# A hybrid encoder layer: scan factors on GpSimd, turns and casts at later places, final sums in two banks

## The chip, the cores and the metric

The kernel runs on one core of a Trainium2 chip. The metric is the device time of one execution in microseconds (us); three executions were timed and the median counts. A further execution was recorded by the hardware profiler, and all durations below come from that one.

The engines of the core are named as in the profile: PE is TensorE (matrix products; PEld is its loading of weights, which overlaps), DVE is VectorE, ACT is ScalarE, POOL is GpSimd, SP is the engine whose queue issues most transfers. Each engine works through its own list of instructions strictly in order, and an instruction that waits holds back everything behind it in its list.

## The reference, cut to what matters

One layer over a prompt of 512 tokens and a sample group of 64 tokens, 1024 wide, in float32:

```python
h = x + W_out [ GDN(n) ; DiffAttn(n) ],  n = rmsnorm(x)      # gated-delta scan, 4 heads of 128
h = h + MemCrossAttn(rmsnorm(h), mk, mv)                     # mk = m @ wk, mv = m @ wv, m = rmsnorm(mem), 256 tokens
h = h + W2 relu(W1 rmsnorm(h))^2                             # 1024 -> 4096 -> 1024
y = rmsnorm_final(h)

# one chunk of the scan, S is the recurrent state of a head
vn = u_c - w_c @ S
o  = qg_c @ S + qk_c @ vn
S  = S * gl_c + kd_c.T @ vn
oa = rmsnorm(o, gdn_norm) * silu(z)                          # a row norm of every head's output, then the gate
```

The queries and keys of the scan are l2-normed rows; the outputs include the memory keys and values, the state and the two rows of caches.

## The kernel before, in words

Everything is held transposed, with features on the 128 partitions and the 576 tokens in the free dimension, and every large product is made of three: weights and inputs are split into a high part in a rounded format (`wh`, `u`) and a low part that holds the rest (`wl`). ACT casts the high part, DVE subtracts to get the low part. Products accumulate in banks of PSUM: three banks `pr` for the large projections, two `ba` for turns (transposes) and small products, and one each of `gs`, `g0` and `g1`, which the scan and its preparation use.

The stages follow each other in the program: norm and input projection; the gated-delta part (`gdn_prep`, `gdn_scan`, `gdn_scan_sample`, some 130 to 290 us into the execution) with the projections of the difference attention as other work for PE beside it; the difference attention (`diff_head`); memory keys and values; output projection; memory attention; the feed-forward layer (`ff1_pair` for its first product, a Strassen-like scheme with seven products of half size); the final norm.

A tile framework schedules the instructions: from the order in which they are written, priorities (`tc.high_priority`) and estimated costs it lays out one list for each engine, so an instruction written early may stand late in its engine's list. `tc.issue_after(x)` asks for a place behind instruction x; `tc.keep_in_program_order` pins one. Where a tile has one buffer (`on`, `r`, `vn`; `on` and `r` even share it) or one bank (`gs`), its next use waits for the last reader.

What the change touches:

- `gdn_prep` (lines 672 to 716) makes for each of five chunks (0 to 3 of the prompt with four blocks, 4 of the sample with two) the row sums `s8` of squared keys and queries, their power -1/2 on POOL (`rpow`, line 208), and from them `nk`, `rq`, `rq2` on DVE (lines 711 to 713), tiny tiles of 128x4. It also solves a triangular system by levels of products in the banks `g0` and `g1` (lines 749 to 783): each level goes PE, ACT (line 762), DVE (763), PE, DVE (770, 771), ACT (769) and back to PE.
- `gdn_scan` (810 to 843) runs the recurrence of one chunk, then `normed` (797 to 808): ACT squares the output that stands in bank `gs` (801), DVE sums the rows (802), makes the factor (803, 804), POOL takes its power (208), DVE multiplies (806) and scales the output out of the bank into `on` (808). Then PE turns `on` back in bank `gs` (`gs<-ident,on`) and DVE applies the gate (842). All of this is written before the preparation of the chunk after next.
- `diff_head` ends with the factor of its own norm (lines 1103 and 1104) inside `finish`.
- The memory keys: a loop over two weights and two halves f; each half makes eight products of 256 tokens in two `pr` banks. For the keys, each half is then turned back (lines 1158 to 1165) through four fillings of a `ba` bank, `ba<-ident,u`, each split by ACT (1131) and DVE (1132).
- `split` (1422 to 1428) casts and subtracts weights of the second feed-forward product: `w2h` on ACT (1426), `w2l` on DVE (1427). The first of them are cast while `ff1_pair(1)` runs, whose partial products are copied out of their banks by `keep` on ACT (1462).
- `final_roots` (1570 to 1581) sums squares over the features with products against a column of ones, `ba<-ones,accq` and `ba<-ones,tm`, then root and scaling.

## Time and profile before

| | us |
|---|---|
| timed runs, median (lowest to highest) | 979.41 (978.93 to 979.56) |
| the profiled execution | 979.89 |
| its span, first to last instruction | 978.2 |
| PE busy | 960.9 |
| PEld busy | 889.0 |
| DVE busy | 691.4 |
| ACT busy | 537.4 |
| POOL busy | 57.5 |
| moved by DMA | 96.01 MB, mean 98 GB/s |

Read it so: a busy time is the time in which an engine had at least one instruction under way. The profiled execution is 1.7 us longer than its span (start and end lie outside), and 0.48 us longer than the median of the timed runs. Of the span, 17.3 us are without PE, and 7.9 of these fall behind the end of the last product at 970.34 us, when the results are scaled and stored. In a row of the timeline the columns are start, duration, engine, line, operation, output and inputs, shape, and in brackets how long the engine had idled before and what ended that. A row of the waits gives the waiting engine and line, what it waited for, and total us, number and longest wait.

### The profile page before, as it was taken

Reading aid. Unit: us, or ns where it says so; the run is one execution under the profiler, and the core shown is the slowest. Engines: PE = TensorE matmul, PEld = TensorE weight load, DVE = VectorE, ACT = ScalarE, POOL = GpSimd, SP = SyncE. Lnnn points to the kernel's source line nnn. Section 1 sums busy time; section 2 is a strip of 40 time slices with the busy share of each in tenths; the row PEclk is TensorE's granted clock in tenths of the full one; section 3 lists DMA queues with packets and bytes.
Section 4 is the critical chain, followed back from the end, with each engine's and each line's share of the span. In section 5 each row is a group of like instructions: output and inputs, shape, how many; then the busy total and the mean of one; then the engine's idle time right before and its main releaser. Section 6 shows DMA issues by size and latency. Waiting matters only on the chain.

```text
span 978.2 us, 16971 instructions
## 1 busy us (share of the span) xinstructions
PE 960.9 (98%) x6399; PEld 889.0 (91%) x6399; DVE 691.4 (71%) x1540; ACT 537.4 (55%) x1218; POOL 57.5 (6%) x125
## 2 busy tenths in 40 slices
PE   9999999999999999999999999999999999999996
PEld 7999999898888878999999998999999999999996
DVE  6655777867767676666657797567867779978674
ACT  7665785444557675445445567665544445545444
POOL 3441020101000000000000000000000000000000
PEclk9999999999999999999999999999999999999998
DMA  7432432121654656341121423322222223233202
GB/s 216 124 124 76 114 105 66 33 55 40 179 132 132 231 159 197 86 130 44 52 58 44 141 70 93 87 87 86 87 87 86 86 87 87 86 88 86 65 23 97
DMA packets 124915, 96.01 MB, mean 98 GB/s; under 512 B 6204, under 2 KB 112846, under 8 KB 124322
## 3 DMA queue, kind: packets, MB, share of 16 engines
q1 hardware_dynamic: 124466, 94.28, 33.2%
q8 instruction: 50, 0.82, 0.3%
q10 hardware_dynamic: 368, 0.66, 0.2%
q14 instruction: 31, 0.25, 0.1%
HBM read 79.93 MB, written 9.75 MB: 92 GB/s over the span
## 4 chain that ended last, share of the span: by engine, by line
PE 86%; DVE 5%; ACT 3%; issue 2%; DMA 2%; POOL 1%; POOLq 0%; ACTq 0%; DVEq 0%; SPq 0%
PE pr L107 53%; PE g L107 11%; PE ba L107 10%; PE gs L107 6%; PE ba L113 3%; PE g L113 2%; DMA raw<-in_w_ff_dram 1%; DMA r<-in_w_ff_dram 1%; POOL tg L208 1%; DVE wl L162 1%; DMA raw<-in_w_mem_o_dram 1%; ACT wh L161 0%; DVE w L1326 0%; PE gs L113 0%; DVE on L808 0%
## 5 line engine op out<-in xcount | busy, mean ns | idle before, releaser
L107 PE MATMUL pr<-u,wh 128*128 128x320 f32 (+2 forms) x1240 | 326.5, 341 | 1.4 <-DVE zr L195 0.9
L107 PEld LDWEIGHTS pr<-u,wh 128*128 128x128 f32 x1240 | 211.9, 188 | 16.9 <-DVE zr L195 1.1
L107 PE MATMUL pr<-u,wl 128*128 128x256 f32 (+1 forms) x816 | 225.8, 301 | 0.0
L107 PEld LDWEIGHTS pr<-u,wl 128*128 128x128 f32 x816 | 150.0, 189 | 2.2 <-DVE wl L388 0.2
L162 DVE TENSOR_TENSOR wl<-raw,wh 128x1024 fp32r<-128x1024 f32 x65 | 79.5, 1223 | 56.0 <-ACT wh L161 55.8
L161 ACT CAST wh<-raw 128x1024 fp32r<-128x1024 f32 x65 | 68.2, 1050 | 59.9 <-PE pr L107 43.9
L107 PE MATMUL pr<-u,w2h 128*128 128x320 f32 (+1 forms) x384 | 98.5, 340 | 0.0
L1426 ACT CAST w2h<-r 128x512 fp32r<-128x512 f32 x56 | 34.7, 620 | 89.0 <-PE pr L107 85.8
L107 PE MATMUL pr<-f,w2h 128*128 128x320 f32 (+1 forms) x288 | 74.4, 341 | 0.2 <-DVE u L1513 0.2
L107 PEld LDWEIGHTS pr<-u,w2h 128*128 128x128 f32 x384 | 65.0, 188 | 4.5 <-ACT u L1509 0.3
L107 PE MATMUL pr<-u,w2l 128*128 128x256 f32 (+1 forms) x256 | 65.1, 295 | 0.0
L1511 DVE TENSOR_TENSOR u<-u,pr 128x256 f32<-128x256 f32 x96 | 42.4, 450 | 17.0 <-PE pr L107 16.3
L107 PE MATMUL ba<-u,wl 128*128 128x288 f32 x360 | 53.0, 296 | 0.9 <-ACT keep L1462 0.9
L107 PEld LDWEIGHTS pr<-f,w2h 128*128 128x128 f32 x288 | 48.7, 188 | 4.2 <-issue 1.4
L107 PEld LDWEIGHTS ba<-u,wl 128*128 128x128 f32 x360 | 49.2, 188 | 1.7 <-ACT keep L1462 1.6
L107 PE MATMUL pr<-f,w2l 128*128 128x256 f32 (+1 forms) x192 | 48.8, 295 | 0.0
L107 PEld LDWEIGHTS pr<-u,w2l 128*128 128x128 f32 x256 | 46.9, 188 | 1.5
L208 POOL TENSOR_TENSOR tiny<-tiny,nhalf 128x1 f32<-128x1 f32 (+4 forms) x10 | 9.1, 913 | 643.4 <-DVE tiny L1579 531.5
L1427 DVE TENSOR_TENSOR w2l<-r,w2h 128x512 fp32r<-128x512 f32 x56 | 38.5, 688 | 11.2 <-ACT w2h L1426 10.9
L107 PE MATMUL pr<-wh,u 128*128 128x512 f32 x128 | 41.4, 398 | 0.0
L1471 ACT ACTIVATE c<-c 128x288 f32<-128x288 f32 x48 | 20.6, 443 | 29.5 <-DVE c L1470 29.5
L107 PEld LDWEIGHTS pr<-f,w2l 128*128 128x128 f32 x192 | 35.2, 188 | 1.1
(551 smaller groups left out, 2022.2 us busy)
## 6 DMA issues: line engine op xcount, KB each, us to landing
raw<-in_w_ff_dram SPq DMA_DIRECT2D x36, 512.0 KB
raw<-in_w_in_dram SPq DMA_DIRECT2D x28, 512.0 KB
r<-in_w_ff_dram SPq DMA_DIRECT2D x56, 256.0 KB
raw<-in_w_mem_k_dram SPq DMA_DIRECT2D x8, 512.0 KB
raw<-in_w_mem_v_dram SPq DMA_DIRECT2D x8, 512.0 KB
raw<-in_w_out_dram SPq DMA_DIRECT2D x8, 512.0 KB
raw<-in_w_mem_q_dram SPq DMA_DIRECT2D x8, 512.0 KB
raw<-in_w_mem_o_dram SPq DMA_DIRECT2D x8, 512.0 KB
```

The lines of the kernel that those rows point to most:

```text
L107: i = nc.tensor.matmul(out, lhsT, rhs, start=start, stop=stop, skip_group_check=skip_group_check)
L113: i = nc.tensor.transpose(out, in_, ident[:n, :n])
L161: A.copy(wh, raw)
L162: V.tensor_tensor(wl, raw, wh.bitcast(F32), ALU.subtract)
L208: G.tensor_tensor(out, in_, bc(nhalf[: in_.shape[0], 0:1], list(in_.shape)), ALU.pow)
L1426: A.copy(wh, src)
L1427: V.tensor_tensor(wl, src, wh.bitcast(F32), ALU.subtract)
L1471: A.activation(c, c, AF.Relu)
L1511: V.tensor_tensor(am, am, b, ALU.add)
```

## The change

Five edits, none of which changes what is computed:

1. In `gdn_prep` the three tiny operations for `nk`, `rq`, `rq2` go from DVE to POOL, directly behind the power.
2. In `normed` the two operations before the power and the one behind it go from DVE to POOL; `normed` becomes a generator that stops before the scaling. `gdn_scan` returns the rest (scaling, turn, gate) as `finish`, and the caller runs it after the preparation of the next chunk has been written; for chunk 3 at once. The sample's scan stops at the same point.
3. In `diff_head` the factor's first operation goes to POOL, and for the last head both are written before `finish`. That last `finish` moves from behind the memory keys into the first half of the memory values.
4. The turns of the memory keys are written inside the next half's product loop (at kc = 1) instead of behind their own half.
5. The non-urgent `split`s of the second feed-forward weights get `issue_after` the last subtraction of `ff1_pair(1)`; and the last sums with `more` go to a bank of their own, with one more small DVE operation (`scalar_tensor_tensor`) that adds the two.

```diff
--- before.py
+++ after.py
@@ -684,10 +684,15 @@
         if c == 0:
             turned.update(summed=nc.cur_bb.bb.instructions[-1])
         V.tensor_scalar(s8, s8, EPS, None, ALU.add)
-        rpow(r8, s8)
         brk = tiny([P, nb], "tg")
         V.reciprocal(brk, s8[:, :nb])
         V.tensor_tensor(brk, brk, be, ALU.mult)
+        nk, rq2 = tiny([P, nb], "tg"), tiny([P, nb], "tg")
+        rq = r8[:, nb:]
+        rpow(r8, s8)
+        G.tensor_tensor(nk, s8[:, :nb], r8[:, :nb], ALU.mult)
+        G.tensor_scalar(rq, rq, P ** -0.5, None, ALU.mult)
+        G.tensor_tensor(rq2, rq, rq, ALU.mult)
 
         if c in grows:
             bg = v4(grows[c], nb)
@@ -706,11 +711,6 @@
         KQ4, vb4 = sb("KQ"), sb("vb")
         KQ = KQ4[:, :nb]
         V.tensor_tensor(KQ, bkq, gam, ALU.mult)
-        nk, rq2 = tiny([P, nb], "tg"), tiny([P, nb], "tg")
-        rq = r8[:, nb:]
-        V.tensor_tensor(nk, s8[:, :nb], r8[:, :nb], ALU.mult)
-        V.tensor_scalar(rq, rq, P ** -0.5, None, ALU.mult)
-        V.tensor_tensor(rq2, rq, rq, ALU.mult)
         bv = each(tr, vblk)
         vb = vb4[:, :nb]
         V.tensor_tensor(vb, bv, nk.unsqueeze(2).to_broadcast(wide), ALU.mult)
@@ -800,10 +800,11 @@
         for R, src in parts:
             A.activation(out[R], src, AF.Square)
         V.tensor_reduce(so, out, AX.X, ALU.add)
-        V.tensor_tensor(so, so, q["rq2"], ALU.mult)
-        V.tensor_scalar(so, so, 1.0 / P, EPS, ALU.mult, ALU.add)
+        G.tensor_tensor(so, so, q["rq2"], ALU.mult)
+        G.tensor_scalar(so, so, 1.0 / P, EPS, ALU.mult, ALU.add)
         rpow(co, so)
-        V.tensor_tensor(co, co, q["rq"], ALU.mult)
+        G.tensor_tensor(co, co, q["rq"], ALU.mult)
+        yield
         for R, src in parts:
             V.tensor_tensor(out[R], src, co[R].unsqueeze(2).to_broadcast(list(src.shape)), ALU.mult)
 
@@ -837,10 +838,15 @@
         b = each(lambda o, h: mm(o, q["kd"][:, h, :], vn[:, h, :]), "ba")
         S = next_state(c, S, b)
         on = sb("on", 1)
-        normed(q, 4, [(slice(0, P), bo)], on)
-        bt = each(lambda o, h: tr(o, on[:, h, :]))
-        V.scalar_tensor_tensor(cq, bt, gn, zs[:, :, L], ALU.mult, ALU.mult)
-        return S
+        norm = normed(q, 4, [(slice(0, P), bo)], on)
+        next(norm)
+
+        def finish():
+            next(norm, None)
+            bt = each(lambda o, h: tr(o, on[:, h, :]))
+            V.scalar_tensor_tensor(cq, bt, gn, zs[:, :, L], ALU.mult, ALU.mult)
+
+        return S, finish
 
     def gdn_scan_sample(q, S):
 
@@ -882,8 +888,10 @@
         yield
         on4 = sb("on", 1)
         on = on4[:, :nb]
-        normed(q, nb, [(R, bo[R, :, i, :]) for i, R in enumerate(own)], on)
+        norm = normed(q, nb, [(R, bo[R, :, i, :]) for i, R in enumerate(own)], on)
+        next(norm)
         yield
+        next(norm, None)
         bt = each(lambda o, i: tr(o, on[:, i, :]), P)
         out = on4[:, nb:].rearrange("p b n -> p (b n)").rearrange("p (h t) -> p h t", h=H)
         V.scalar_tensor_tensor(out, bt[:, : H * DEC].rearrange("p (h t) -> p h t", h=H), gn, zsample, ALU.mult, ALU.mult)
@@ -899,14 +907,17 @@
                 A.copy(mhi, src)
                 V.tensor_tensor(mlo, src, mhi.bitcast(F32), ALU.subtract)
 
-    S = None
+    S, behind = None, lambda: None
     prepared = [gdn_prep(*chunks[0])]
     for c, _, L in chunks[:4]:
         prepared.append(gdn_prep(*chunks[c + 1]))
         if c == 0:
             turn_memory()
             project_z()
-        S = gdn_scan(c, L, prepared[c], S)
+        behind()
+        S, behind = gdn_scan(c, L, prepared[c], S)
+        if c == 3:
+            behind()
     nc.sync.dma_start(o_gdn_p[0, 0].rearrange("h k v -> k h v"), S)
     oa = pair(2, F32R)
     for h in range(H):
@@ -1099,9 +1110,16 @@
             A.activation(pr[1][:, :P], po, AF.Square, accum_out=so[:, t : t + 1])
             A.copy(on[:, t, :], po)
 
+        def factors():
+            G.tensor_scalar(so, so, 1.0 / P, EPS, ALU.mult, ALU.add)
+            rpow(co, so)
+
+        if h == H - 1:
+            factors()
+
         def finish():
-            V.tensor_scalar(so, so, 1.0 / P, EPS, ALU.mult, ALU.add)
-            rpow(co, so)
+            if h < H - 1:
+                factors()
             V.tensor_tensor(on, on, co.unsqueeze(2).to_broadcast([P, 5, P]), ALU.mult)
             b, b2 = bank(), bank()
             for t in range(4):
@@ -1134,6 +1152,21 @@
     mkv = pair(1, F32R)
     mkT, mv, tokens = view(mkv, 0, KT, NMEM), view(mkv, 1, 2, D), view(e3, 1, 2, D)
     mkl, mvl = lows("At0", "At1", "Dt0", "Dt1"), lows("Y0", "Y1", "B1", "B1")
+    turn_keys = lambda: None
+
+    def key_turns(f, dst):
+        def turn_keys():
+            for i in range(2):
+                b = bank()
+                for j in range(2):
+                    m = 4 * f + 2 * i + j
+                    for t in range(2):
+                        tr(b[:, j * 256 + t * P : j * 256 + (t + 1) * P], dst[:, t, m * P : (m + 1) * P])
+                m = 4 * f + 2 * i
+                split_turned(mkT[:, m : m + 2, :], mkl[m // 2].rearrange("p (j n) -> p j n", j=2), b)
+
+        return turn_keys
+
     for w, out in ((w_mem_k, o_mk), (w_mem_v, o_mv)):
         dst = tokens
         for f in range(2):
@@ -1141,6 +1174,10 @@
             bs = [bank("pr") for _ in range(2)]
             for kc in range(4):
                 wt = split_weights(w[0, 256 * kc : 256 * kc + 256, fs], [P, 2, 512])
+                if kc == 1:
+                    turn_keys()
+                    if out is o_mv and f == 0:
+                        finish()
                 for k in (2 * kc, 2 * kc + 1):
                     for t in range(2):
                         ts_ = slice(t * P, (t + 1) * P)
@@ -1154,18 +1191,8 @@
                 if out is o_mv:
                     A.copy(mv[:, t, fs], dst[:, t, fs])
                     V.tensor_tensor(mvl[2 * t + f], dst[:, t, fs], mv[:, t, fs].bitcast(F32), ALU.subtract)
-            if out is o_mk:
-                for i in range(2):
-                    b = bank()
-                    for j in range(2):
-                        m = 4 * f + 2 * i + j
-                        for t in range(2):
-                            tr(b[:, j * 256 + t * P : j * 256 + (t + 1) * P], dst[:, t, m * P : (m + 1) * P])
-                    m = 4 * f + 2 * i
-                    split_turned(mkT[:, m : m + 2, :], mkl[m // 2].rearrange("p (j n) -> p j n", j=2), b)
             nc.sync.dma_start(out[0, 0].rearrange("(b p) h d -> p b (h d)", p=P)[:, :, fs], dst[:, :, fs])
-            if out is o_mk and f == 1:
-                finish()
+            turn_keys = key_turns(f, dst) if out is o_mk else lambda: None
             if out is o_mv and f == 0:
                 ob = pair(5, F32R)
                 for h in range(H):
@@ -1422,7 +1449,7 @@
     def split(src, tag, bufs, urgent):
         shape = list(src.shape)
         wh, wl = (ft(tag + x, shape, bufs, F32R) for x in "hl")
-        with tc.high_priority() if urgent else ExitStack():
+        with tc.high_priority() if urgent else tc.issue_after(put_last[1]):
             A.copy(wh, src)
             V.tensor_tensor(wl, src, wh.bitcast(F32), ALU.subtract)
         return wh, wl
@@ -1433,6 +1460,7 @@
         return split(raw, "w2", 3, urgent)
 
     NG, SCALED = 8, 5
+    put_last = {}
 
     def ff1_pair(p, sx):
         ws = parts.pop(p)
@@ -1492,6 +1520,7 @@
         put(1, N1, s3, s5)
         product(4, x, False)
         put(1, N0, x[:, :NH], None)
+        put_last[p] = nc.cur_bb.bb.instructions[-1]
         if p + 1 < 2 * NG:
             split_pair(p + 1)
         if p + 2 < 2 * NG:
@@ -1573,10 +1602,14 @@
         r, r2 = tiny([P, 8]), tiny([P, 8])
         for i, t in enumerate(ts):
             q0, n = QT[t]
-            mm(b[:, t : t + 1], accs[0][:, q0 : q0 + n], ones[:, 0:1], stop=more is None, pin=pin and i == 0)
-            if more is not None:
-                mm(b[:, t : t + 1], more[:, q0 - 256 : q0 - 256 + n], ones[:, 0:1], start=False)
+            mm(b[:, t : t + 1], accs[0][:, q0 : q0 + n], ones[:, 0:1], pin=pin and i == 0)
         V.tensor_scalar(r[:, c], b[:, c], 1.0 / D, EPS, ALU.mult, ALU.add)
+        if more is not None:
+            b = bank()
+            for t in ts:
+                q0, n = QT[t]
+                mm(b[:, t : t + 1], more[:, q0 - 256 : q0 - 256 + n], ones[:, 0:1])
+            V.scalar_tensor_tensor(r[:, c], b[:, c], 1.0 / D, r[:, c], ALU.mult, ALU.add)
         rpow(r2[:, c], r[:, c])
         return r2
 
```

How the lists of the engines stand before and after at three places (a row is line, operation, output and inputs, shape; the lines of the changed kernel are some numbers higher).

First, DVE's list at the norm of chunk 0, `tg` being the factor and `on` the output. Before:

```order
L802 TENSOR_REDUCE tg_1892<-on_1891 128x4
L771 TENSOR_TENSOR Dt_214_1517<-Dt_214_1517,g_228_1582 128x16x16
L803 TENSOR_TENSOR tg_1892<-tg_1892,tg_1334 128x4
L676 TENSOR_TENSOR kd_1914<-g_274_1909,kdc 128x512
L804 TENSOR_SCALAR tg_1892<-tg_1892 128x4
L806 TENSOR_TENSOR tg_1893<-tg_1893,tg_1279 128x4
L808 TENSOR_TENSOR on_1891<-gs_1879,tg_1893 128x512
```

Now:

```order
L802 TENSOR_REDUCE tg_1892<-on_1891 128x4
L676 TENSOR_TENSOR kd_1907<-g_273_1902,kdc 128x512
L809 TENSOR_TENSOR on_1891<-gs_1879,tg_1893 128x512
L783 TENSOR_SCALAR X_1515<-g_234_1614 64x4x64
L679 TENSOR_REDUCE tg_1901<-B_275_1909 128x4
```

Three tiny rows left DVE's list, and the scaling (line 809) stands two places behind the row sum instead of six; the tiny rows follow each other in POOL's list, around the power of line 208.

Second, PE's list ahead of the turn of chunk 3, `gs<-ident,on`. Before:

```order
L107 MATMUL pr_3365<-u_94,wl_3362 128x256
L107 MATMUL pr_3365<-u_94,wh_3361 128x512
L107 MATMUL g_410_2450<-Y_395_2397,X_2396 128x128
L107 MATMUL pr_3365<-u_94,wl_3362 128x256
L113 MATMUL gs_2511<-ident,on_2501 128x128 x4
```

Now:

```order
L107 MATMUL ba_2492<-vn_2481,kd_2126 128x128
L113 MATMUL ba_2644<-ident,u_78 128x128 x2
L107 MATMUL g_406_2431<-Y_394_2390,X_2389 128x128
L113 MATMUL ba_2684<-ident,u_78 128x128 x2
...
L113 MATMUL ba_2719<-ident,zr_2716 128x128 x2
L113 MATMUL g_408_2438<-ident,Y_394_2390 128x128
L107 MATMUL g_408_2438<-Dt_395_2391,B_407_2436 128x128
L113 MATMUL ba_2750<-ident,zr_2748 128x128 x2
...
L113 MATMUL gs_2511<-ident,on_2501 128x128 x4
L107 MATMUL pr_3363<-u_93,wh_3359 128x512
```

Before, the turn stood among the products of the next projection, `pr`. Now it stands ahead of the first of them, behind turns, small products and levels of the solve (`...` marks rows left out).

Third, PE's list at the last turns of the memory keys, `ba<-ident,u`, and of the last head, `ba<-ident,an`. Before:

```order
L113 MATMUL ba_4211<-ident,u_76 128x128 x4
L113 MATMUL ba_4295<-ident,u_76 128x128 x4
L107 MATMUL pr_4322<-wh_4326,u_1250 128x512 x2
L107 MATMUL pr_4322<-wl_4327,u_1250 128x512
...
L113 MATMUL ba_4302<-ident,u_76 128x128 x4
L107 MATMUL pr_4323<-wh_4344,u_1250 128x512
L113 MATMUL ba_4313<-ident,an_3948 128x128 x4
```

Now:

```order
L107 MATMUL pr_4299<-wl_4303,u_1250 128x512
L113 MATMUL ba_4324<-ident,u_76 128x128 x4
L113 MATMUL ba_4331<-ident,u_76 128x128 x4
L107 MATMUL pr_4298<-wh_4320,u_1250 128x512 x2
L107 MATMUL pr_4298<-wl_4321,u_1250 128x512
...
L113 MATMUL ba_4339<-ident,an_3948 128x128 x4
```

Before, three fillings of `ba` followed each other closely and a fourth soon after; now they come in pairs, with a projection's products between the pairs, and the head's turn last.

## The prediction

> **What bounds the kernel now.** I read the page first: its line of busy times, then the chain of work that ended last.
>
> ```profile
> PE 960.9 (98%) x6399; PEld 889.0 (91%) x6399; DVE 691.4 (71%) x1540; ACT 537.4 (55%) x1218; POOL 57.5 (6%) x125
> PE 86%; DVE 5%; ACT 3%; issue 2%; DMA 2%; POOL 1%; POOLq 0%; ACTq 0%; DVEq 0%; SPq 0%
> ```
>
> PE is the bound: 960.9 of a span of 978.2 us, and the change leaves PE's number of products as it is. All that can be won are the 17.3 us without PE, and what can be lost is new waiting of PE. So the next view is the table of busy time in windows of 20 us, of which these are the windows that lack PE and that the edits touch (columns: window, length, busy time of PE, PEld, DVE, ACT, POOL with numbers of instructions, granted clock, DMA).
>
> ```profile
> 120.00:140.00 20.00, 19.40 (x137) 18.05 (x136) 13.86 (x38) 18.26 (x32) 3.90 (x3) 1.00 0.43 142
> 160.00:180.00 20.00, 19.07 (x156) 16.85 (x155) 14.11 (x41) 8.63 (x18) 3.25 (x4) 1.00 0.15 40
> 180.00:200.00 20.00, 19.64 (x153) 18.50 (x152) 18.29 (x50) 8.62 (x20) 2.71 (x2) 1.00 0.15 41
> 220.00:240.00 20.00, 19.45 (x151) 17.53 (x149) 13.86 (x44) 6.92 (x20) 2.32 (x3) 1.00 0.10 27
> 240.00:260.00 20.00, 18.91 (x126) 16.69 (x125) 16.50 (x45) 12.47 (x35) 1.27 (x1) 1.00 0.75 199
> 280.00:300.00 20.00, 19.20 (x123) 17.45 (x122) 14.90 (x53) 11.20 (x41) 1.84 (x2) 1.00 0.36 103
> 360.00:380.00 20.00, 18.92 (x88) 15.34 (x88) 14.42 (x18) 11.85 (x16) 0.00 (x0) 1.00 0.54 171
> 580.00:600.00 20.00, 19.11 (x141) 18.55 (x140) 14.52 (x26) 15.34 (x37) 0.00 (x0) 1.00 0.42 119
> 600.00:620.00 20.00, 19.68 (x132) 18.43 (x131) 15.08 (x27) 13.54 (x33) 0.00 (x0) 1.00 0.45 132
> ```
>
> These nine lack 0.60, 0.93, 0.36, 0.55, 1.09, 0.80, 1.08, 0.89 and 0.32 us. That caps the gains: 4.33 us in the gated-delta windows (120 to 300 us), 1.08 us at the memory keys, 1.21 us in the feed-forward layer. The clock is granted in full in all of them. The view of waits says who ends these gaps.
>
> ```profile
> PE gs L113 <- DVE on L808: 1.3, 2, 0.8
> PE gs L107 <- DVE on L808: 0.7, 1, 0.7
> PE ba L113 <- DVE At L1132: 1.1, 1, 1.1
> PE ba L107 <- ACT keep L1462: 1.2, 2, 0.9
> DVE tg L711 <- POOL tg L208: 3.2, 3, 1.5
> DVE tg L806 <- POOL tg L208: 2.8, 3, 1.1
> ```
>
> Three waits of PE are for the scaling of a scan's norm (line 808), one is for the keys' split, two are for `keep`. And DVE itself stood 6.0 us for POOL's powers.
>
> **The scan's factors and last steps.** The timeline of chunk 0's norm, from the squares to the turn:
>
> ```profile
> 168.76 0.60 ACT L801 ACTIVATE on<-gs 128x512 f32<-128x512 f32 x1 [0.15 <-PE gs L107]
> 169.02 0.97 PEld L107 LDWEIGHTS ba<-vn,kd 128*128 128x128 f32 x8
> 169.54 0.68 DVE L802 TENSOR_REDUCE tg<-on 128x4 f32<-128x512 f32 x1
> 170.46 0.16 DVE L803 TENSOR_TENSOR tg<-tg,tg 128x4 f32<-128x4 f32 x1
> 171.14 0.16 DVE L804 TENSOR_SCALAR tg<-tg 128x4 f32<-128x4 f32 x1
> 171.38 1.01 POOL L208 TENSOR_TENSOR tg<-tg,nhalf 128x4 f32<-128x4 f32 x1 [10.12 <-DVE tg L804]
> 172.43 0.16 DVE L806 TENSOR_TENSOR tg<-tg,tg 128x4 f32<-128x4 f32 x1 [1.12 <-POOL tg L208]
> 172.62 0.69 DVE L808 TENSOR_TENSOR on<-gs,tg 128x512 f32<-128x512 f32 x1
> 173.37 0.55 PE L113 MATMUL gs<-ident,on 128*128 128x128 f32 x3 [0.75 <-DVE on L808]
> ```
>
> Between the end of the row sum (170.22) and the scaling (172.62) lie 2.40 us: two tiny operations on DVE that stand behind other work there, the power, a third. DVE loses 34 tiny rows (20 of two inputs, 14 of one) at about 0.16 us, 5.4 us in all, plus the 6.0 us of waiting. DVE is not the bound, so this is worth only what PE waits for it.
>
> The trace has no multiplication of 128x4 on POOL. The nearest rows by lines:
>
> ```profile
> L208 POOL TENSOR_TENSOR tg<-tg,nhalf 128x4 f32<-128x4 f32 x5 | 5.3, 1067 | 52.3 <-DVE tg L804 47.6 <-DVE tg L686 4.7
> L461 POOL COPY cst<-p 128x3 f32<-128x3 f32 x11 | 8.1, 733 | 23.0 <-ACT p L322 23.0
> L462 POOL COPY cst<-p 128x3 f32<-128x3 f32 x11 | 2.0, 183 | 1.0 <-ACT p L323 1.0
> ```
>
> A copy of 128x3 takes 0.73 us after a pause of POOL and 0.18 us right behind another; a power of 128x4 takes 1.07. So one tiny operation lies between 0.18 and 1.07 us. I take 0.6 for the first (a pause precedes it) and 0.25 for each later one, near the copies, since neither has the power's arithmetic: 0.6 + 0.25 + 1.07 + 0.25 = 2.2 us against 2.40 now. The chain from row sum to scaling stays as long as it was; by the bounds it is 1.6 to 4.3 us. GPSIMD Engine Reference of the Trainium skill (section Engine selection) speaks against the move: elementwise work belongs on VectorE, with GpSimd about twice as slow for two inputs. By it each moved operation would take an estimated 0.32 us, the chain 2.0, and the slower rival below would lose its price.
>
> What does change is DVE's list: at chunks 0 to 2 the scaling (809) now stands two or three places behind the row sum, so DVE stands idle for it, 2.2 less 0.7 to 1.1 us of work between, some 1.3 us each. Queued behind are steps of the other chunk's solve and preparation. At chunks 0 to 2 PE has projection products (`pr`) beside these; behind the outputs of chunk 0, PE's list to its turn holds some 5 us of work (ten products of scan and solve at about 0.24 each, by the 0.97 us of the row's eight loads, two to a product; ten turns at half of that; eighteen shorter ones), against 0.15 + 0.60 + 0.18 + 0.68 + 2.2 + 0.7 = 4.5 us of chain. I leave 0.1 of the 0.75 us there and 0.2 of the 0.55 at chunk 2: **-1.0**. The 0.60 and 0.36 us at 120 to 140 and 180 to 200 us lie where DVE waited for the powers of the preparation; I give back 0.4 of the 0.96: **-0.4** (bounds 0 and -0.96). At the sample's norm the wait of 0.69 us for line 808 has as many products ahead as chain: **-0.2**.
>
> Chunk 3 is the bad place, and it speaks against the change. Today's gap near its norm is another one:
>
> ```profile
> 243.63 1.27 POOL L208 TENSOR_TENSOR tg<-tg,nhalf 128x4 f32<-128x4 f32 x1 [13.76 <-DVE tg L804]
> 244.19 0.42 DVE L195 TENSOR_TENSOR zr<-pr,zr 128x256 f32<-128x256 f32 x1
> 244.67 0.50 PE L107 MATMUL pr<-u,wh 128*128 128x512 f32 x1 [0.85 <-DVE zr L195]
> ```
>
> PE waits 0.85 us for a bank that `zr` (195) empties late. Now the scaling of chunk 3 stands directly ahead of `zr` on DVE, and the turn directly ahead of the first `pr` on PE. From the last product of the outputs to the turn the chain is 4.5 us plus the hop to PE, 4.6. PE has behind those outputs four products `ba<-vn,kd` (0.97 us as above), four of the solve (0.24 each) and some thirteen turns (0.12 each), and little more: 3.5 us. PE is short of 1.1 us. Ahead of it, I take 0.4 us as lost at the hops of the solve and the scan, which had projection products between them. The 0.85 goes: **+0.65**. The bounds: -0.85, if other waits of the solve fall into the same time, and +3.6, if the tiny operations cost as much as a power (2.1 us more) and the levels of the solve are bare (0.85 more). That power took 1.27 us here, while DVE worked beside it, and 1.01 at chunk 0, while DVE waited; the same page (section Key points) says that GpSimd shares its SBUF interfaces with VectorE and collides with instructions of two SBUF inputs, and the two rows agree; by it chunk 3's chain would be an estimated 0.25 us longer, and the sum -2.15.
>
> **Memory keys.**
>
> ```profile
> 361.76 0.65 PE L113 MATMUL ba<-ident,u 128*128 128x128 f32 x4 [1.08 <-DVE At L1132]
> ```
>
> The fourth filling waits 1.08 us for one of two `ba` banks. In the new list two fillings, then twenty products `pr`, then two fillings stand: no third one waits. The turns read copies (1153) made well ahead. The last head's turn moves behind its power by more. **-1.0** (bounds -1.08 and +0.5, if the turned half, now written among the next half's products, meets a bank that the difference attention still holds).
>
> **Second feed-forward weights.**
>
> ```profile
> 589.39 0.62 ACT L1426 CAST w2h<-r 128x512 fp32r<-128x512 f32 x1 [2.07 <-DMA r<-in_w_ff_dram]
> 591.25 0.40 ACT L1462 COPY keep<-ba 128x288 f32<-128x288 f32 x1
> 591.70 1.06 PE L107 MATMUL ba<-u,wl 128*128 128x288 f32 x6 [0.89 <-ACT keep L1462]
> 607.37 1.34 PE L107 MATMUL ba<-u,w 128*128 128x288 f32 x8 [0.27 <-ACT keep L1462]
> ```
>
> ACT stands 2.07 us for the weights of a cast (1426), the `keep` comes late, PE waits 0.89. The edit is meant for this, but the lists show that it does not reach ACT: the same cast stands between the same two rows there. The instruction it names is DVE's, and only DVE's subtractions move behind it, by some 10 us, with the buffers `r` they free and three loads that wait for these; the products that need them come 10 us later still. So the 0.89 us stay. ACT's `keep` at 606 us does stand earlier, ahead of two casts of weights: the 0.27 goes, **-0.3** (bounds -0.6 and +0.5, where a copy that now stands behind frees a `pr` bank late at 615 us).
>
> **Final sums.**
>
> ```profile
> 968.67 0.30 PEld L107 LDWEIGHTS ba<-ones,tm 128*128 128x128 f32 x2 [0.16 <-ACT tm L1201]
> 969.59 0.36 PE L107 MATMUL ba<-ones,tm 128*128 128x1 f32 x2
> 969.99 0.16 DVE L1579 TENSOR_SCALAR tiny<-ba 128x3 f32<-128x3 f32 x1 [1.87 <-PE ba L107]
> ```
>
> Six sums before and six now, 0.23 us apart (968.67 to 969.59 in four steps). Two of them now run ahead of the turns, so PE's weight load no longer waits 0.16 us for `tm`; the added DVE row replaces the one on the path, which moves into the 1.87 us of idling. **-0.15** (bounds -0.3 and +0.2).
>
> **The sum.** -1.0 - 0.4 - 0.2 + 0.65 - 1.0 - 0.3 - 0.15 = -2.4 us on the profiled execution (979.89, span 978.2): 977.5. The timed median is 0.48 us lower; from 979.41 the same step gives 977.0.
>
> **The rivals.**
>
> - The waits only change place. For it: chunk 3's list, and that the scan is one chain of hops whatever PE does beside it. Against it: the keys' 1.08 us have nothing to do with the scan. The scan then takes 1.6 us more than in the sum, so that its gains are gone, 978.6, and with the keys' gain at half 979.1.
> - Slower, by one mechanism: a tiny operation on POOL costs as much as the power, 1.0 us. The chain is then 4.2 us instead of 2.2. DVE, standing in order at the scaling, is idle 3.3 us at each chunk; PE's turns of chunks 0, 2, 3 and the sample come 2.0 us later with nothing left to cover it, 8 us, less some 3 us that the projections behind cover when they come in between: +5 against the sum, 982.0. It decides from about 0.6 us for each operation. For it: the power row of 1.07, and 0.73 for a copy. Against it: the copies of 0.18.
> - Everything is covered, because DVE is freer and its later work no longer stands behind powers: the chunk 3 term is -0.85 instead of +0.65 and the 0.96 us go whole: 974.9.
> - The casts go later on ACT after all, and the 0.89 us go too: 976.1.
>
> **How the numbers follow.** Forecast 0.50, own range 975.2 to 978.5; waits moved 0.17; slower 0.16; all covered 0.12; casts 0.05. What a measurement of this kernel can tell from no change is about 0.2%, 2.0 us. Faster by more than that (below 977.45): 0.12 + 0.05, 0.36 of the forecast's 0.50, and 0.02 of the moved waits: 0.55. Slower (above 981.37): 0.16, and 0.02 of the moved waits: 0.18. Between: 0.27. The range takes in the moved waits, part of the slower case and most of the covered one: 974.0 to 981.2.
>
> **What would show it.** Right: no wait of PE for the scaling at chunks 0 and 2 (now 0.75 and 0.55), none for the keys' split at 361 us, DVE's waits for POOL gathered at line 809, an unchanged wait of 0.89 us for `keep` near 590 us, PE short by about 1.5 us ahead of chunk 3's turn. Wrong: tiny POOL rows above 0.6 us; PE idle over 4 us in 160 to 300 us; or a new gap at the memory values. Most in doubt is the stretch of chunk 3.

## The result and the profile after

| | before | changed |
|---|---|---|
| median of 22 runs each, us | 979.69 | 978.34 |
| lowest to highest | 978.48 to 981.85 | 977.08 to 979.61 |
| span of the profiled execution | 978.2 | 976.5 |

The ratio is 0.9986 with a 95% interval of 0.998 to 0.9992: 1.4 us faster, clear of no change, but under the 2.0 us that was named as what can be told. The forecast was 2.4 us faster; the sign and the range held, while three of its larger terms did not. By the span from first to last instruction the gain is larger: the 22 executions have a median span of 976.05 us, and the kernel before had 977.8 to 978.2 in the three series of the experiments below. The time outside the span was 1.7 to 2.0 us in these executions of the kernel before and 1.9 to 3.3 in the changed one; why is not known. The page of the changed kernel begins:

```profile
span 976.5 us, 16991 instructions
PE 961.3 (98%) x6399; PEld 890.0 (91%) x6399; DVE 689.2 (71%) x1507; ACT 537.4 (55%) x1218; POOL 64.9 (7%) x159
```

PE did the same work. So the windows of 20 us tell again where it stood still (third number: PE busy; what is missing to 20 us is idle time).

```profile
120.00:140.00 20.00, 19.71 (x140) 18.54 (x139) 13.90 (x34) 17.64 (x32) 5.90 (x9) 1.00 0.52 159
160.00:180.00 20.00, 19.90 (x163) 17.72 (x162) 12.69 (x31) 9.98 (x20) 2.40 (x7) 1.00 0.11 27
180.00:200.00 20.00, 19.69 (x151) 18.76 (x149) 17.46 (x39) 8.76 (x19) 4.01 (x8) 1.00 0.25 63
220.00:240.00 20.00, 18.06 (x146) 16.34 (x145) 14.79 (x41) 7.44 (x20) 3.56 (x9) 1.00 0.10 27
240.00:260.00 20.00, 19.31 (x134) 16.89 (x133) 14.87 (x43) 12.81 (x40) 1.61 (x4) 1.00 0.62 171
280.00:300.00 20.00, 19.54 (x121) 17.36 (x120) 14.79 (x48) 11.43 (x38) 2.41 (x5) 1.00 0.35 94
340.00:360.00 20.00, 19.19 (x99) 15.12 (x98) 15.53 (x34) 14.11 (x34) 1.36 (x2) 1.00 0.48 146
580.00:600.00 20.00, 19.98 (x150) 19.59 (x148) 13.87 (x25) 16.46 (x39) 0.00 (x0) 1.00 0.29 84
600.00:620.00 20.00, 19.95 (x136) 19.07 (x135) 16.11 (x30) 12.91 (x31) 0.00 (x0) 1.00 0.57 169
```

PE idle by stage, summed from these views of both kernels (with the windows that are not shown):

| stage | before | changed |
|---|---|---|
| 120 to 220 us, preparation, chunks 0 and 1 | 1.89 | 0.75 |
| 220 to 260, chunks 2 and 3 | 1.64 | 2.63 |
| 260 to 300, sample | 1.16 | 0.59 |
| 340 to 380, memory keys | 1.09 | 0.81 |
| 580 to 620, second feed-forward weights | 1.21 | 0.07 |

Gains of 1.1 us at the first chunks and at the feed-forward weights and of 0.6 at the sample, a loss of 1.0 in the stretch of chunks 2 and 3, and at the keys only 0.3 of the 1.0 expected. At chunk 2's turn PE still waits for the scaling, 0.56 us where it was 0.55:

```profile
227.88 0.66 PE L113 MATMUL gs<-ident,on 128*128 128x128 f32 x4 [0.56 <-DVE on L809]
```

The timeline ahead of chunk 3's outputs shows the loss:

```profile
234.96 0.37 ACT L779 COPY Y<-g 64x256 f32<-64x256 f32 x1
235.47 0.65 PE L107 MATMUL g<-X,Y 128*64 128x64 f32 x8 [0.64 <-ACT Y L779]
236.41 0.41 DVE L783 TENSOR_SCALAR X<-g 64x256 f32<-64x256 f32 x1
236.87 0.71 PE L107 MATMUL gs<-on,X 128*128 128x128 f32 x4 [0.39 <-DVE X L783]
238.60 0.49 PE L107 MATMUL g<-Y,X 128*128 128x128 f32 x2 [0.23 <-DVE Y L763]
```

PE waits 1.3 us here in all. Each of these steps of the solve and of the scan (the hops) waits for the one before, on another engine, with no projection product between. The turn itself waits for nothing, and GpSimd is quick:

```profile
242.58 0.69 DVE L802 TENSOR_REDUCE tg<-on 128x4 f32<-128x512 f32 x1 [0.31 <-ACT on L801]
243.35 0.20 POOL L803 TENSOR_TENSOR tg<-tg,tg 128x4 f32<-128x4 f32 x1 [11.12 <-DVE tg L802]
243.64 0.19 POOL L804 TENSOR_SCALAR tg<-tg 128x4 f32<-128x4 f32 x1
243.91 1.02 POOL L208 TENSOR_TENSOR tg<-tg,nhalf 128x4 f32<-128x4 f32 x1
245.01 0.20 POOL L806 TENSOR_TENSOR tg<-tg,tg 128x4 f32<-128x4 f32 x1
245.24 0.69 DVE L809 TENSOR_TENSOR on<-gs,tg 128x512 f32<-128x512 f32 x1 [0.23 <-POOL tg L806]
245.99 0.66 PE L113 MATMUL gs<-ident,on 128*128 128x128 f32 x4
```

At the keys a new wait, for the low part of a block of value weights, stands in place of the old one:

```profile
355.13 0.83 DVE L1123 TENSOR_TENSOR an<-an,ta 128x640 f32<-128x640 f32 x1 [1.97 <-POOL ta L208]
357.14 1.22 DVE L162 TENSOR_TENSOR wl<-raw,wh 128x1024 fp32r<-128x1024 f32 x1
358.41 0.49 PE L107 MATMUL pr<-wl,u 128*128 128x512 f32 x1 [0.71 <-DVE wl L162]
```

And near 590 us, where ACT's list is what it was, ACT's wait for the load `r` is 0.93 us instead of 2.07 and PE waits for nothing.

```profile
588.69 0.62 ACT L1453 CAST w2h<-r 128x512 fp32r<-128x512 f32 x1 [0.93 <-DMA r<-in_w_ff_dram]
590.55 0.40 ACT L1490 COPY keep<-ba 128x288 f32<-128x288 f32 x1
591.10 1.63 PE L107 MATMUL ba<-u,wl 128*128 128x288 f32 x11
```

### The profile page after: what moved, and what is told of

It is laid out like the page before. It is cut to its first block, busy times and chain, and to the rows that moved or that the text cites. A ratio compares the mean times of both kernels' runs of the same rounds, so it can differ in the third digit from the quotient of the medians.

```text
span 976.5 us, 16991 instructions
## 1 busy us (share of the span) xinstructions
PE 961.3 (98%) x6399; PEld 890.0 (91%) x6399; DVE 689.2 (71%) x1507; ACT 537.4 (55%) x1218; POOL 64.9 (7%) x159
## 4 chain that ended last, share of the span: by engine, by line
PE 55%; DVE 3%; issue 2%; DMA 1%; ACT 1%; POOLq 0%; POOL 0%; ACTq 0%; DVEq 0%
PE pr L107 33%; PE ba L107 11%; PE g L107 7%; PE gs L107 4%; DMA raw<-in_w_ff_dram 1%; PE ba L113 1%; DVE wl L162 1%; DVE u L1353 1%; DMA raw<-in_w_mem_o_dram 0%; DVE u L1215 0%; ACT wh L161 0%; ACT u L1592 0%; DVE u L1217 0%; DVE w2l L1353 0%; DVE f L1368 0%
## 5 line engine op out<-in xcount | busy, mean ns | idle before, releaser
L1540 DVE TENSOR_TENSOR u<-u,pr 128x256 f32<-128x256 f32 x96 | 42.4, 451 | 17.3 <-PE pr L107 16.6
```

The costliest lines, as they stand in the source:

```text
L1540: V.tensor_tensor(am, am, b, ALU.add)
```

## The experiments

Twelve kernels were run, with 5 to 11 runs each, and compared with the kernel before on the same chip. An interval is about 0.9 us to either side (1.3 for the kernels with 5 and 6 runs), so the idle time of PE in the windows decides where the medians cannot. It comes from one execution of each kernel. Between kernels that are alike in a stage it repeats to 0.2 us in the windows of the table; the exceptions are 240 to 260 us and 580 to 620 us.

**One part alone.** First the scan's part on the kernel before, with the same three operations of `gdn_prep` on `G` (GpSimd; `V` is VectorE). The cuts of the edits leave lines out at `...`.

```diff
-        V.tensor_tensor(so, so, q["rq2"], ALU.mult)
-        V.tensor_scalar(so, so, 1.0 / P, EPS, ALU.mult, ALU.add)
+        G.tensor_tensor(so, so, q["rq2"], ALU.mult)
+        G.tensor_scalar(so, so, 1.0 / P, EPS, ALU.mult, ALU.add)
         rpow(co, so)
-        V.tensor_tensor(co, co, q["rq"], ALU.mult)
+        G.tensor_tensor(co, co, q["rq"], ALU.mult)
+        yield
...
+        behind()
+        S, behind = gdn_scan(c, L, prepared[c], S)
```

> The kernel before with only the scan's part (factors of the preparation and of the norms on GpSimd, last steps behind the next chunk). Theory: most of what the scan gained at the norms of chunks 0 and 2 went at chunk 3; PE short of 3.5 to 4.5 us in 120 to 300 us (4.7 before), waits at the hops ahead of chunk 3's outputs as in the changed kernel, the stalls at 360 us (1.08) and 590 us (0.89) as before; time -0.3 to -0.9 us, ratio 0.9991 to 0.9997. Rival (the scan carries the whole gain): ratio 0.9985 or lower.

Measured: 979.82 against 979.91, ratio 1.0001 (0.9992 to 1.001). PE idle in 120 to 300 us was 4.55 (4.69 before), 1.94 of it in 220 to 240. The theory's reason held (gained at the norms, lost at chunk 3), but not its -0.3 us: the scan's part gives nothing that can be told. It also did something at the keys, where nothing was edited: VectorE's list came out differently there, the last head's scaling stands earlier among the low parts `wl`, and the wait of 1.08 us for the bank gave way to one for `wl`, with 0.72 us idle in 340 to 380 us (1.09 before, 0.81 in the changed kernel).

```profile
358.43 0.50 PE L107 MATMUL pr<-wl,u 128*128 128x512 f32 x1 [0.62 <-DVE wl L162]
```

Then the later turns of the keys alone, with the last head's `finish` where it was:

```diff
+                if kc == 1:
+                    turn_keys()
...
             if out is o_mk and f == 1:
                 finish()
+            turn_keys = key_turns(f, dst) if out is o_mk else lambda: None
```

> The kernel before with only the memory keys' turns later; the last head's final step stays behind the keys. Theory A (in the changed kernel the gain was lost because VectorE stood 2.0 us for GpSimd's power at the last head's step, which now sits between the splits of the value weights): here that step stands elsewhere, the wait of 1.08 us goes and no wait for wl appears, -0.8 to -1.2 us. Theory B (the splits of the turned keys themselves delay the value weights' low parts): PE waits 0.5 to 1.2 us for wl of line 162, time within 0.3 us of before.

Measured: 980.21, ratio 1.0003 (0.9994 to 1.0012). The gain did not come, and neither theory had the place right: the turn of the last head, now next to use the `ba` bank, waited in its stead, for the scaling that stands behind GpSimd's power.

```profile
360.38 0.83 DVE L1105 TENSOR_TENSOR an<-an,ta 128x640 f32<-128x640 f32 x1 [1.28 <-POOL ta L208]
361.36 0.63 PE L113 MATMUL ba<-ident,an 128*128 128x128 f32 x4 [1.27 <-DVE an L1105]
```

So the 0.3 us at the keys of the changed kernel is not shown to come from the keys' edit: alone it gained nothing, and the scan's part alone gave as much there.

Third, the later casts alone:

```diff
-        with tc.high_priority() if urgent else ExitStack():
+        with tc.high_priority() if urgent else tc.issue_after(put_last[1]):
```

> The kernel before with only the later casts of the first second-layer weights. Theory (the later subtractions on VectorE hold back one load of 256 KB, so that the load that ACT waits for lands about 1 us earlier): the wait of 0.89 us for keep at 590 us shrinks to under 0.2, and that of 0.27 at 607 us goes; time -0.9 to -1.3 us, ratio 0.9987 to 0.9991. Rival (the loads landed earlier by chance or by what came before): 0.89 stays, time -0.2 to -0.4 us.

Measured: 978.67, ratio 0.9988 (0.9979 to 0.9997). PE idle in 580 to 620 us: 0.10. By the medians this part alone gives nearly the whole of the change. One caution: without it that idle time varied from execution to execution (1.21, 0.62, 0.94, 0.24 and 0.81 us in five profiles, of kernels that differ elsewhere); with it, it was 0.05 to 0.19 in eight. So in idle time it is worth some 0.7 us on average.

Fourth, the final sums alone:

```diff
+        if more is not None:
+            b = bank()
...
+            V.scalar_tensor_tensor(r[:, c], b[:, c], 1.0 / D, r[:, c], ALU.mult, ALU.add)
```

> The kernel before with only the last sums in two banks. Theory: from the start of the last twelve products pr<-f,u to GpSimd's last power 4.63 us before and 4.44 here, all else as before: -0.2 us, ratio 0.9998. Rival (the second small VectorE operation lies on the path): 4.6 to 4.8 us, no gain.

Measured: 979.87, ratio 0.9999 (0.9991 to 1.0008), too small to tell by the runs; by the profile 4.45 us from 964.52, the start of the last twelve products, to the power at 968.97, against 4.63 before and 4.44 in the changed kernel.

**Why the casts' part works.** In the window from 582 to 592 us SP's queue issued these loads of `r`, first in the kernel before, then in the changed one (columns: start of the first, time to the end of the last, queue, line, operation, count):

```profile
582.68 8.45 SPq L1432 DMA_DIRECT2D r<-in_w_ff_dram  x4
```

```profile
584.72 0.92 SPq L1459 DMA_DIRECT2D r<-in_w_ff_dram  x2
```

Before, a third of these loads was issued at 584.69 us, while the first two were awaited: its buffer came free when VectorE subtracted the first low part. With that subtraction at 601 us instead, the third load is not issued until 601.62. The load that the cast waits for is the first: before, it was issued at 582.68 and landed 6.69 us later; in the changed kernel it was issued at 584.72 and had landed when the cast began at 588.69, 4.0 us later. It started 2 us later and came 0.7 us sooner.

Whether the third load is to blame was tried by putting one more load there:

```diff
+            if (g, m) == (1, 2):
+                spare = dp.tile([P, 4, P], F32, tag="spare", name="spare")
+                with tc.issue_after(nc.cur_bb.bb.instructions[-3]):
+                    nc.sync.dma_start(spare, w_ff2[0, :512, 3 * P : 4 * P].rearrange("(k p) n -> p k n", p=P))
```

> The changed kernel with one more load of 256 KB, read from the second-layer weights into a spare place in DRAM that nobody reads, issued right behind the load r for the third cast, where the kernel before issued its next load. Theory (competition of loads made ACT wait near 590 us): ACT's cast waits 1.5 to 2.3 us for r again, keep comes late, and PE waits 0.5 to 1.0 us; time +0.4 to +1.1 us over the changed kernel. Rival (the order of VectorE's subtractions did it): no wait of PE at 590 us, time as the changed kernel within 0.2 us.

```profile
584.89 0.67 SPq L1653 DMA_DIRECT2D spare<-in_w_ff_dram  x1
588.84 0.62 ACT L1453 CAST w2h<-r 128x512 fp32r<-128x512 f32 x1 [1.87 <-DMA r<-in_w_ff_dram]
591.15 1.06 PE L107 MATMUL ba<-u,wl 128*128 128x288 f32 x6 [0.68 <-ACT keep L1490]
```

Measured: 978.92, ratio 0.9995 (0.9986 to 1.0003), 0.6 above the changed kernel's median; the intervals overlap, so the profile decides. The awaited load, issued at 583.92, was in flight for 4.90 us, the cast waits 1.87 us again, and PE 0.68. PE is idle for 0.73 us in 580 to 620, against 0.05 to 0.19 in the eight kernels without the extra load. From 580 to 592 us the lists of PE, ACT and VectorE are those of the changed kernel, so it is competition of loads, and not the order of VectorE's subtractions, that brings the stall back. The extra load differs from the old third one in writing to DRAM.

**Inside the scan's part.** First the last steps at once, with the factors still on GpSimd:

```diff
-        behind()
         S, behind = gdn_scan(c, L, prepared[c], S)
-        if c == 3:
-            behind()
+        behind()
```

> The changed kernel with the last steps of each chunk of the prompt written at once, as before, and the factors on GpSimd. Theory (the placing behind the next chunk is what gains at chunks 0 to 2 and what strips chunk 3 of projection products): waits of 0.5 to 1 us at the turns of chunks 0 and 2 return, the stretch ahead of chunk 3's outputs loses under 1 us instead of 2; time within 0.8 us of the changed kernel, PE short of 4 to 5 us in 120 to 300 us. Rival (GpSimd's factors strip chunk 3): the loss of 2 us there stays and the turns wait again, +1 us or more.

Measured: 977.73, ratio 0.9981 (0.9972 to 0.9989); PE idle 3.22 us in 120 to 300. Better than the changed kernel: the loss ahead of chunk 3 is gone (0.55 in 220 to 240 instead of 1.94), and of the waits at the turns only chunk 1's grew, by 0.3 us. The theory held on chunk 3 and was wrong on the turns: those of chunks 0 and 2 wait for nothing worth naming here, with the factors on GpSimd and no later placing.

Then the factors back on VectorE, with the later placing kept:

```diff
         rpow(r8, s8)
-        G.tensor_tensor(nk, s8[:, :nb], r8[:, :nb], ALU.mult)
-        G.tensor_scalar(rq, rq, P ** -0.5, None, ALU.mult)
-        G.tensor_tensor(rq2, rq, rq, ALU.mult)
+        V.tensor_tensor(nk, s8[:, :nb], r8[:, :nb], ALU.mult)
+        V.tensor_scalar(rq, rq, P ** -0.5, None, ALU.mult)
+        V.tensor_tensor(rq2, rq, rq, ALU.mult)
```

The factors of `normed` and `diff_head` likewise.

> The changed kernel with the factors back on VectorE and the last steps still behind the next chunk. Theory (GpSimd's 0.2 us for each and VectorE's 0.16 make chains of equal length, and VectorE is not the bound): PE short of 3.5 to 5 us in 120 to 300 us, time within 0.7 us of the changed kernel. Rival (the move off VectorE is what gains): +0.8 us or more, with VectorE waiting for GpSimd's powers 5 us or more in all.

Measured: 980.06, ratio 1.0008 (0.9999 to 1.0017), 1.7 us over the changed kernel; PE idle 6.54. The rival held. But the edit left `nk`, `rq` and `rq2` directly behind the power, where VectorE now waited for it ahead of work that PE needed: 1.49 us at one place (0.29 in the changed kernel).

```profile
133.47 1.16 PE L107 MATMUL g<-u 128*128 128x128 f32 x8 [1.49 <-DVE Y L704]
```

So that kernel does not separate the engine from the place of these three rows. The placing was therefore also tried alone on the kernel before, all factors where they were:

```diff
         V.tensor_tensor(co, co, q["rq"], ALU.mult)
+        yield
...
+        behind()
+        S, behind = gdn_scan(c, L, prepared[c], S)
```

> The kernel before with only the last steps placed behind the next chunk, all factors on VectorE in their old places. Theory (the placing alone costs, GpSimd's factors gain): PE short of 5 to 6 us in 120 to 300 us against 4.7 before, time +0.3 to +1.3 us. Rival (the loss seen with factors on VectorE came from their earlier place in the preparation): 4.0 to 4.8 us, time within 0.3 us of before.

Measured: 978.34, ratio 0.9986 (0.9977 to 0.9994); PE idle 3.56. Both the theory and the rival were wrong: the placing without GpSimd's factors gains 1.1 us of idle time in this stretch, and the factors without the placing gain 1.5 (the kernel with the steps at once against 4.7; both kernels hold the sample's later scaling). Against the 6.54 us of the kernel just shown, 3.56 also says what the early place of `nk`, `rq` and `rq2` costs when they are on VectorE: some 3 us. Together the two edits gain little: 3.97 to 4.88 us in five executions with the same scan. The windows 220 to 240 us, with the placing alone, the steps at once and both (the last from the kernel with the pinned scaling below, whose lists are the changed kernel's but for one row):

```profile
220.00:240.00 20.00, 19.51 (x154) 17.72 (x154) 14.46 (x46) 8.23 (x23) 2.27 (x3) 1.00 0.10 27
```

```profile
220.00:240.00 20.00, 19.45 (x150) 17.06 (x149) 14.31 (x40) 7.46 (x20) 3.77 (x9) 1.00 0.10 25
```

```profile
220.00:240.00 20.00, 18.07 (x145) 16.37 (x145) 14.75 (x41) 7.44 (x20) 3.58 (x9) 1.00 0.10 27
```

PE's lists say why. From the first product of chunk 3 with the state to its turn, the projection products `pr` in between are 42 in the kernel before, 30 with the placing alone, 16 with the steps at once, and 1 in the changed kernel. With 16 or more of them this window loses about 0.5 us, with one of them 1.9, of which 0.56 is chunk 2's turn. They are the work that fills the hops here.

Whether it is the placing of chunk 2 alone was tried with the steps of chunks 2 and 3 written at once:

```diff
-        if c == 3:
+        if c >= 2:
             behind()
+            behind = lambda: None
```

> As the kernel of both pieces, but the last steps of chunks 0 and 1 stand behind the next chunk and only those of chunks 2 and 3 are written at once. Theory (chunk 1's placing gains 0.3 us at 180 to 200 us, chunk 2's placing strips chunk 3): PE short of 2.8 to 3.3 us in 120 to 300 us, the same as with all at once or 0.3 us better. Rival (any placing behind the next chunk uses up the projection products ahead of chunk 3): 2 us of waiting in 220 to 240 us return, 4 us or more in 120 to 300.

Measured: 977.13, ratio 0.9977 (0.9968 to 0.9986), idle 4.17, 2.07 of it in 220 to 240: the rival held, the placing of chunks 0 and 1 alone already uses up the products (7 left). This kernel also holds the pinned scaling that comes next.

**The last head's scaling.** In the changed kernel VectorE stands 1.97 us for GpSimd's power at this step, just ahead of the `wl` that PE waits for. First it was written later:

```diff
                 if kc == 1:
                     turn_keys()
-                    if out is o_mv and f == 0:
-                        finish()
+                if kc == 3 and out is o_mv and f == 0:
+                    finish()
```

> The changed kernel with the last head's final step two weight blocks later (kc 3 instead of 1) in the first half of the memory values. Theory A (VectorE standing for the power makes wl late): the wait of 0.71 us for wl near 358 us goes, time -0.5 to -1.0 us. Theory B (the splits of the keys do): wait stays at 0.5 or more, time within 0.3 us of the changed kernel.

Measured: 978.4, ratio 0.9987 (0.9978 to 0.9996), and it tested nothing: the scaling kept its early place in VectorE's list, with its wait of 1.97 us at 354.74, and PE's wait of 0.69 for `wl` stayed. A step written later need not be scheduled later. So it was pinned instead:

```diff
                 if kc == 1:
+                    low_part = nc.cur_bb.bb.instructions[-1]
                     turn_keys()
                     if out is o_mv and f == 0:
-                        finish()
+                        with tc.issue_after(low_part):
+                            finish()
```

> The changed kernel with one VectorE instruction moved: the scaling of the last head (an, line 1123), which waits 1.97 us for GpSimd's power, stands behind the low parts of the second block of value weights. All other lists are unchanged. Theory A (VectorE, standing for the power, makes wl late): PE's wait of 0.71 us for wl near 358 us goes, VectorE no longer waits for GpSimd there, time -0.6 to -1.1 us against the changed kernel. Theory B (the casts and splits of the turned keys do it): wait stays at 0.5 us or more.

```profile
340.00:360.00 20.00, 19.99 (x105) 16.23 (x104) 16.01 (x36) 15.08 (x38) 1.36 (x2) 1.00 0.48 155
360.00:380.00 20.00, 20.00 (x96) 16.57 (x95) 13.11 (x16) 11.44 (x15) 0.00 (x0) 1.00 0.74 233
```

Measured: 976.45 (6 runs), ratio 0.9967 (0.9955 to 0.998). PE's wait is gone, 0.8 us by the windows, by the move of one VectorE row; the lists of PE, ACT, GpSimd and SP are the changed kernel's, row for row. Theory A held on the wait. The median fell by more than was expected, 1.9 us below the changed kernel's; the intervals meet at 0.998. In the two profiles the span fell by 0.9 us, 0.6 of it PE's busy time, because 240 to 260 us lost 0.9 us more. What the rest of the median's fall is was not found.

Both findings together, the steps at once and the scaling pinned, in one kernel:

> Last steps of each chunk at once, factors on GpSimd, and the last head's scaling later (both of the earlier pieces). Theory: the gains add, PE short of 3.0 to 3.4 us in 120 to 300 us and under 0.3 in 340 to 380; ratio to before 0.9970 to 0.9978, 2.2 to 2.9 us faster than before. Rival (the later stages are bound by something else, and the wait reappears): no more than the kernel with the steps at once, 0.9981.

Measured: 976.63 (5 runs), ratio 0.9967 (0.9954 to 0.998), span 974.6, idle 3.19 in 120 to 300 us and 0.00 in 340 to 380. It is 3.3 us faster than the kernel before, and its interval meets the changed kernel's at 0.998. The idle times add as the theory had it; the runs cannot tell this kernel from the one with the pinned scaling alone.

## Why the prediction was right, and where it was not

- **That PE bounds it, and only its idle time counts: right.** PE's busy time moved by 0.4 us. In the stages of the table idle time fell by 2.1 us, which is the fall of all idle time (17.3 to 15.2); elsewhere it moved by up to 0.5 us in a window, both ways. The timed median fell by only 1.35 us: in this pair of profiles PE's busy time took back 0.4 of the gain, and the time outside the span, which the prediction took as unchanged, has a median some 0.3 us longer.
- **Tiny operations on GpSimd: right in the chain, too dear for the first.** The first was put at 0.6 us. They took 0.20 us in the norms, also after a pause of 11 us, and 0.26 to 0.32 on average in the preparation. The chain from row sum to scaling was 1.97 us (243.27 to 245.24), where 2.2 was put. So the slower rival, which needed 0.6 us for each, was out. One row in the preparation did take over 0.6 us, a sign that had been named for "wrong". It ran beside a VectorE row and ended 0.05 us after it:

```profile
136.43 0.68 DVE L733 SCALAR_TENSOR_TENSOR B<-lev,At 128x512 f32<-128x512 f32 x1
136.47 0.69 POOL L693 TENSOR_TENSOR tg<-tg,tg 128x4 f32<-128x4 f32 x1
```

At 182.13 us, beside the same VectorE line, such a row took 0.50 us and ended just as soon after it. The page GPSIMD Engine Reference of the Trainium skill names this contention (section Key points: VectorE instructions with two inputs from SBUF, the working memory of the engines), and these rows agree. The chain of chunk 3 does not put it to the test: beside its power of 1.02 us VectorE's rows read one input from a PSUM bank. What the same page gave for the cost (section Engine selection, about twice VectorE's time for two inputs, an estimated 0.32) lies above the norms' rows and at the highest of the preparation's means; the prediction took it for the operations of one input too, where the page does not state it.
- **Turns of chunks 0 and 2, -1.0: 0.8 at chunk 0, none at chunk 2.** 160 to 180 us lost 0.93 and now 0.10, but at chunk 2's turn PE waits 0.56 us as before, which was put at 0.2. The -0.4 for the preparation came as -0.36, and the sample's -0.2 as -0.3.
- **Chunk 3, +0.65: too small.** With chunk 2's turn the stretch of 220 to 260 us was to cost 0.3 and cost 1.0 (1.5 on average over four other executions with the same scan). The step that failed is the 1.1 us put for the turn and 0.4 us for the hops: the turn cost nothing visible, the hops ahead of the outputs some 1.3 us, and one hop of the solve behind them 0.42. The prediction counted the work behind the outputs and not the missing products ahead of them.
- **Memory keys, -1.0: the wait was replaced.** It came out at -0.28, and with a new gap at the memory values, which the prediction had named as a sign of being wrong. VectorE's wait for GpSimd's power, which the sum of this part did not hold, made the next low part late; the pinned scaling, one row moved, shows it. The line "the last head's turn moves behind its power by more" looked at PE and not at VectorE, on which that step stood in front of `wl`.
- **Feed-forward weights, -0.3: a wrong step with the other sign.** "So the 0.89 us stay" was drawn from ACT's unchanged list. The text had the cause in hand, the buffers `r` and the loads that wait for them, and priced it as harmless to later products; it did not consider that a load held back lets the awaited one land sooner. The edit was worth -1.1 us in this pair of profiles, and about -0.7 against the mean of the five without it.
- **Final sums, -0.15: right** (-0.19).

By the windows the turn of chunk 2, chunk 3 and the keys came out 0.35, 0.33 and 0.7 us worse than put, the feed-forward weights 0.8 us better. That errors of opposite sign nearly cancelled, so that the total came out nearer than its terms, was luck.

## What to carry to other kernels

Look at what stands behind a moved step on every engine in its list, and at how many independent products are left between two dependent ones: two edits that each use up the same spare work gain apart and clash together. When a wait is for a load, ask which other loads run beside it, and what frees the buffers that let them start. An edit in the order of writing moves nothing until the engine's list shows it.

## What the runs showed of the hardware

- One load of 256 KB more delayed an awaited load of the same size by about 1 us: it was in flight for 4.90 us with it and 4.0 without, and ACT's cast waited 1.87 us and 0.93.
- GpSimd's tiny operations on 128x4 cost 0.20 us after a pause of 11 us, where a copy of 128x3 after a pause had taken 0.73. Beside a VectorE row with two inputs from SBUF they took up to 0.69 us and ended with that row.
- The same lists did not idle equally where PE waits for a transfer: 240 to 260 us left PE idle for 0.69 to 1.59 us in five executions of the same scan, while 220 to 240 us stayed at 1.93 or 1.94. In the kernel with 1.59 the row below waits for a copy by DMA; in the changed kernel, with 0.69, the same product waits for nothing.

```profile
257.21 0.30 PE L107 MATMUL g<-Dt,qs 128*128 128x128 f32 x1 [0.89 <-DMA Dt<-At]
```
